# State-layer input weights turned by dense 64x64 products, inputs shifted by transfers, output products that ask for one head at a time, wider planner lags

## The chip, the cores and the metric

The kernel runs on one NeuronCore of a Trainium2 chip. The metric is device time in microseconds (us), and lower is better. The engines named here are TensorE (PE, with its weight loads as PEld), VectorE (DVE), ScalarE (ACT), GpSimd (POOL) and SyncE (SP, which issues the transfers). "att", "acc" and "big" are banks of PSUM, where products land.

## The reference

One layer for 256 tokens of width 2048, in float32. The state layer, which the change is about, is one of three mixers that read one projection:

```python
h = rmsnorm(x, norm_mix_pre)
q_na, k_na, v_na, u_ssm, q_mem = split(h @ w_in)
y_na  = neighbourhood_attention(q_na, k_na, v_na, rpb)       # 8 heads x 128
y_ssm = s5_mixer(u_ssm, ...)                                 # 32 groups of 16 channels, 64 complex states
y_mem = memory_cross_attention(q_mem, mem, ...)              # 4 heads x 128
# s5, each direction: bu = u @ b_bar ; h_t = lam_bar * h_(t-1) + bu_t (a scan over 256 steps) ; y = Re(c h)
y = concat(rmsnorm(y_na), rmsnorm(y_ssm), rmsnorm(y_mem))
x = x + rmsnorm(y @ w_out)
x = x + rmsnorm(square(relu(rmsnorm(x) @ w_ff1)) @ w_ff2)
```

## The kernel before

**The weight stream.** All dense weights lie in one stream of 128x1024 chunks (512 KB), in the order of their use. SP loads a chunk into `wraw` (three buffers); ScalarE rounds it to `wh` (conv_high), VectorE forms the rest `wl` (conv_low), and TensorE multiplies with both, three products for each of the reference's. `take` hands TensorE the next columns; it has the chunk two ahead converted, and a conversion issues the load of the chunk three further on. Chunks 0 to 15 are the first part of `w_in`, 16 to 31 `w_mem_kv`, 32 to 79 values, queries and keys of the neighbourhood heads, from 80 on `w_out`, then the MLP. A chunk of `w_mem_kv` is 12 products with the weight as stationary operand (into two banks), then 6 with `memS` as stationary operand.

**The planner.** There is no dynamic scheduler. While the program is written out, a clock for each engine is advanced by estimated costs. The side work lives in generators (`spawn`). At every half chunk `take` calls `tick`, which steps those that are due, and so puts their instructions between the products of the stream. After a step a task is due again when the engine it used is expected to be done plus a lag, `LAG[min(pri, 2)]`. `drain` steps one task until it is done. Every engine then runs its instructions strictly in the order that came out, so a wait of one instruction holds up all behind it on that engine.

**The state layer.** The 256 steps are cut into 64 blocks of four. `g0_evac` writes the input `uT` with VectorE and shifts it into `U4`, whose partitions hold the four steps of a block. For each of four groups `ut`, `prep_b` builds on VectorE the input weights times four powers of lambda (`W`). For each direction `d` it spreads them into `wx` (ScalarE; one half of the channels is zero), turns them on TensorE by 8 transposes of 128x128 (one pass each in the trace) and copies them to `W1T` (ScalarE). `incr` multiplies W1T with U4: 32 products of 128 rows by 32 columns with 64 moving columns, four column strips at a time (`tile_position=(0, 32 * m)`). A float32 product that is no transpose has two records, so an increment shows as x64. `XS` takes the result, `tree` scans it on VectorE, `ssm_out` multiplies with `CC`.

**The attention heads and the output projection.** `att_task` runs one head in steps (scores, softmax, `PT`, values). `na_fin` turns finished heads into `mixn`. The output projection first takes the memory heads (`mixm`, four groups of two chunks), then `drain(nf)` steps the other tasks until all eight heads stand in mixn, then come four groups over mixn.

Of the kernel before, what the change touches and what calls it, by code (L numbers as in the profile page):

```python
# [11 lines left out]
F32 = mybir.dt.float32  # L12
# [15 lines left out]
MEMH = 4  # L28
EPS = 1e-6
LAM_RE_MAX = -1e-4  # L30
NB = S // 4
LEV = 6
SCALE = 128 ** -0.5
# [4 lines left out]
HALF = DFF // 2 // 128  # L38
LASTK = 12
MARGIN = 200.0  # L40
LAG = (1200.0, 2000.0, 800.0)
SH_V = 1e9
SH_G = 500.0
BACK_V, BACK_G, BACK_A, BACK_TREE = 2600.0, 4000.0, 3000.0, 1700.0
# [59 lines left out]
def hybrid_kernel(ctx: ExitStack, tc: tile.TileContext, A: dict, out: bass.AP, dbg=None):  # L104
# [16 lines left out]
    class Engine:  # L121
# [3 lines left out]
        def __getattr__(self, name):  # L125
            f = getattr(self.raw, name)
            e = self.e

            def call(o, *a, **kw):
                n = 1  # L130
                for d in o.shape[1:]:
                    n *= d
                if e == "E":
                    m = a[0].shape[-1]
                    if name == "transpose":
                        c = 110.0
                    elif a[0].dtype == F32R:
                        c = n * 0.4225
                    else:
                        c = max(n, 128) * 1.69 * (0.31 if m == 32 else 1.0) if n > 4 else 110.0  # L140
                elif name == "tensor_reduce":
                    c = 80 + 1.04 * a[0].shape[1] * a[0].shape[2]
                elif e == "A":
                    c = (205 + 0.83 * n + (80 if isinstance(kw.get("scale"), bass.AP) or "bias" in kw else 0)
                         + (186 if "accum_out" in kw else 0))
                elif e == "V":
                    c = (72 if n > 64 else 140) + n * {"tensor_copy": 0.52, "reciprocal": 8.0, "tensor_tensor_scan": 1.04,
                                   "tensor_scalar": 0.76, "memset": 0.3}.get(name, 1.04)
                else:
                    c = 155 + n * {"tensor_scalar": 0.9, "memset": 0.0, "tensor_copy": 1.6}.get(name, 2.1)  # L150
                if e == "V" and n > 64 and name == "tensor_tensor" and any(
                        abs(x.ap[-1][0]) >= 4 for x in (o, a[0]) if x.ap[-1][1] > 1):
                    c += 0.9 * n
                book(e, c)
                return f(o, *a, **kw)  # L155
            return call
# [83 lines left out]
    def live(gen):  # L240
        return any(t[1] is gen for t in tasks)
# [18 lines left out]
            while more and all(clk[e.upper()] - clk["E"] < BACK[e] for e in t[3]):  # L260
                more = step(t)

    def drain(g):
        while live(g):
            me = next(t for t in tasks if t[1] is g)
            was = dict(clk)
            clk["E"] = max(clk["E"], me[2])
            step(me)
            if clk == was:
                for t in list(tasks):  # L270
                    if t is not me:
                        step(t)
                if clk == was:
                    clk["E"] += 500.0
# [383 lines left out]
    uT = a2.tile([128, 4, 256], F32, name="uT")  # L658
    U4 = a2.tile([128, 16, NB], F32, name="U4")

    wx = a2.tile([128, 8, 4, 2, 16], F32, name="wx")
    V.memset(wx.rearrange("p n l j b -> p (n l j b)"), 0.0)

    loaded = {}

    def load_b(ut):
# [5 lines left out]
    def prep_b(ut):  # L672
        yield from until(lambda: ut in loaded and clk["E"] > loaded[ut][1])
        raw = loaded[ut][0]
        w = a2.tile([128, 2, 2, 4, 4, 16], F32, name="W", tag="W", bufs=1)
        par = a2.tile([128, 4, 2, 2, 4], F32, name="par", tag="par", bufs=1)
        for i, x in enumerate((cfr, cfi, lbr, lbi)):
            act(par[:, i], x[:, 8 * ut:8 * ut + 8].rearrange("p (d q) -> p d q", d=2)[:, :, None, :]
                .to_broadcast([128, 2, 2, 4]))
        yield from done("A")  # L680
        for l in range(4):
            o = w[:, :, :, :, l, :]
            src = (w[:, :, :, :, l - 1, :].rearrange("p d c q b -> p (d c q) b") if l
                   else raw.rearrange("p (n b) -> p n b", b=16))
            r_, i_ = (par[:, 2 * min(l, 1) + i].rearrange("p d c q -> p (d c q)")[:, :, None].to_broadcast([128, 16, 16])
                      for i in range(2))
            t = a2.tile([128, 2, 2, 4, 16], F32, name="pt", tag="pt", bufs=1)
            tt(V, t.rearrange("p d c q b -> p (d c q) b"), src, i_, mult)
            tt(V, o.rearrange("p d c q b -> p (d c q) b"), src, r_, mult)
            tt(V, o[:, :, 0], o[:, :, 0], t[:, :, 1], sub)  # L690
            tt(V, o[:, :, 1], o[:, :, 1], t[:, :, 0], add)
            yield True
        yield from done("V")
        act(W0[ut].rearrange("p d c q j b -> p (d c q) j b"),
            w[:, :, :, :, 0, :].rearrange("p d c q b -> p (d c q) b")[:, :, None, :].to_broadcast([128, 16, 2, 16]))
        w0_done.add(ut)
        if ut % 2 == 0:
            XS[ut // 2] = a2.tile([128, 2, 16, NB], F32, name="XS", tag="AB", bufs=2)
        for d in range(2):
            for j in range(2):  # L700
                h = slice(64 * j, 64 * j + 64)
                act(wx[h, :, ::-1 if d == 0 else 1, j, :], w[h, d].rearrange("p c q l b -> p (c q) l b"))
            yield PE
            wt = a2.tile([128, 2, 4, 128], F32, name="W1T", tag="W1T", bufs=2)
            ps2 = [att(), att()]
            for n in range(8):
                PE.transpose(ps2[n // 4][:, n % 4 * 128:(n % 4 + 1) * 128], wx[:, n].rearrange("p l j b -> p (l j b)"),
                             ident)
            for c in range(2):
                act(wt[:, c].rearrange("p q m -> p (q m)"), ps2[c])  # L710
            spawn(incr(ut, d, wt, clk["A"] + MARGIN + LAG[2]), 2, "A")
            yield True

    def incr(ut, d, wt, t0):

        yield from until(lambda: ssm_done and clk["E"] > t0 and (d == 0 or (ut, 0) in xs_part))
        p = att()
        X = p.rearrange("p (c q m) -> p c q m", c=2, q=4)
        for c in range(2):
            for q in range(4):  # L720
                for m in range(4):
                    PE.matmul(X[32 * m:32 * m + 32, c, q, :], wt[:, c, q, 32 * m:32 * m + 32], U4[:, 4 * ut + q, :],
                              start=True, stop=True, skip_group_check=True, tile_position=(0, 32 * m))
        c0 = 8 * (ut % 2) + 4 * d
        act(XS[ut // 2][:, :, c0:c0 + 4, ::-1 if d else 1], X)
        xs_part.add((ut, d))
        yield
# [251 lines left out]
    def g0_evac():  # L979
        b = st_rx["b"]  # L980
        for j in range(2):
            tt(V, qkm[:, 2 * j:2 * j + 2, 0, :], pq[j].rearrange("p (a b) -> p a b", a=2),
               b[:, None, :].to_broadcast([128, 2, 256]), mult)
        yield
        for u in range(4):
            tt(V, uT[:, u].rearrange("p (r c) -> p c r", c=16),
               pu[:, u * 256:(u + 1) * 256].rearrange("p (c r) -> p c r", c=16), b.rearrange("p (c r) -> p c r", c=16),
               mult)
        yield
        for q in range(4):  # L990
            for i in range(4):
                o = U4[32 * i:32 * i + 32, q:16:4, :]
                s = uT[32 * q:32 * q + 32, :, i * NB:(i + 1) * NB]
                if i % 2:
                    G.tensor_copy(o, s)
                else:
                    act(o, s)
            if q < 3:
                yield True
        ssm_done.append(1)  # L1000
        if dbg:
            dbg("uT", uT.rearrange("p a b -> p (a b)"))
        yield
# [93 lines left out]
    acc1 = a1.tile([128, 2, D], F32, name="acc1", tag="x16", bufs=2)  # L1097
    mixn = a1.tile([128, 2, NAH, 256], F32R, name="mixn", tag="x16", bufs=2)

    def na_fin():  # L1100
        for h in range(NAH):
            yield from wait_for(naT[h])
            yield from split_task(mixn[:, 0, h, :], mixn[:, 1, h, :], yna[:, h, :], col(V_NA, h))

    def na_rms():
        yield from wait_for(nf)
# [3 lines left out]
    nf = spawn(na_fin(), pri=1)  # L1110
    nr = spawn(na_rms(), pri=1)

    def out_group(mh, ml, n):

        po = [acc(), acc()]
        for k in range(n):
            wh, wl = take(4)
            for t in range(2):
                s = slice(t * 128, (t + 1) * 128)
                mm_tok(po[t], mh[:, k, s], ml[:, k, s], wh, wl, start=(k == 0), stop=(k == n - 1))  # L1120
        return po
# [4 lines left out]
    for o in range(4):  # L1126
        po = out_group(mixm[:, 0], mixm[:, 1], 4)
        for t in range(2):
            act(acc1[:, t, quarter(o)], po[t], AF.Copy, scale=st_rx["mo"][:, t:t + 1])
    drain(nf)  # L1130

    mixs = {}

    def glu():
        yH, yL = yHL["H"], yHL["L"]
# [35 lines left out]
    for o in range(4):  # L1171
# [2 lines left out]
            gl = glu()  # L1174
        if o == 2:
            drain(nr)
        p1 = spawn(post1(o, out_group(mixn[:, 0], mixn[:, 1], NAH)), 1)
    drain(p1)
    drain(gl)
    A2.close()  # L1180
# [363 lines left out]
```

## Time and profile before

| | |
|---|---|
| median of 3 runs (lowest, highest) | 1140.99 us (1138.22, 1141.76) |
| the profiled execution, its span | 1140.01 us, 1138.2 us |
| busy share PE, DVE, ACT, POOL | 98%, 63%, 51%, 9% |
| bytes read from HBM | 209.02 MB |

The program is the same in every run. Of the span, about 417 us are the mixers and the output projection, which the change touches, and about 704 us the MLP, which it leaves as it was. In the rows below a product is written out<-in by the program's names; "U" is U4, "x" is x1. Loads of `x` and `gpost` are 256 KB each.

### The profile page before, as it was taken

What the parts mean: (1) busy time and instruction counts of PE and PEld (TensorE: products, weight loads), DVE (VectorE), ACT (ScalarE), POOL (GpSimd) and SP (SyncE); (2) the same over time, 40 slices, a digit from 0 to 9 for tenths busy, and PEclk for the clock granted to TensorE, in tenths of its full rate; (3) what the DMA queues carried; (4) which work ended last, traced back from release to release, by engine and by line L of the source; (5) the groups of instructions that cost most, each with busy time, mean ns of one, the idle gap of its engine ahead of it and who ended that gap; (6) DMA issues with size and microseconds to landing.
All of it is one profiled execution on the core that took longest, in us unless ns stands there. A gap on an engine that the chain in (4) does not pass through costs nothing.

```text
span 1138.2 us, 18307 instructions
## 1 busy us (share of the span) xinstructions
PE 1111.2 (98%) x7208; PEld 957.6 (84%) x7208; DVE 721.3 (63%) x1069; ACT 578.3 (51%) x900; POOL 104.8 (9%) x179
## 2 busy tenths in 40 slices
PE   8999999899999999999999999999999999999996
PEld 8988899799788878888888888888888888888885
DVE  6777588888876776866664444445666665445454
ACT  6567856636655464644455434434444444344341
POOL 1780000020110161000000000000000000001010
PEclk9999999999999999999999999999999999999999
DMA  9876444345455766666666666666666666666663
GB/s 302 291 254 184 127 145 142 114 140 166 135 148 179 249 188 181 189 191 191 187 186 193 189 189 186 186 187 192 193 186 189 191 191 187 186 198 195 193 209 129
DMA packets 62726, 212.31 MB, mean 187 GB/s; under 512 B 7216, under 2 KB 9776, under 8 KB 62640
## 3 DMA queue, kind: packets, MB, share of 16 engines
q1 hardware_dynamic: 62352, 211.05, 60.5%
q8 instruction: 56, 0.92, 0.3%
q14 instruction: 30, 0.25, 0.1%
q10 hardware_dynamic: 288, 0.09, 0.0%
HBM read 209.02 MB, written 2.10 MB: 185 GB/s over the span
## 4 chain that ended last, share of the span: by engine, by line
PE 83%; DVE 7%; DMA 3%; ACT 3%; issue 2%; POOL 1%; SPq 0%; DVEq 0%; POOLq 0%; ACTq 0%
PE acc L155 74%; PE big L155 6%; PE att L155 4%; DMA wraw<-in_w_dram 3%; DVE wl L155 3%; ACT wh L155 1%; DVE ps L155 1%; DVE W L155 1%; DVE XS L155 1%; ACT P L155 0%; DVE pt L155 0%; DVE mn L155 0%; DVE P L155 0%; POOL x L155 0%; DMA gpost<-in_post_dram 0%
## 5 line engine op out<-in xcount | busy, mean ns | idle before, releaser
L155 DVE TENSOR_TENSOR wl<-wraw,wh 128x1024 fp32r<-128x1024 f32 (+1 forms) x372 | 458.3, 1234 | 374.9 <-ACT wh L155 374.3
L155 ACT ACTIVATE wh<-wraw 128x1024 fp32r<-128x1024 f32 (+1 forms) x372 | 391.4, 1054 | 440.5 <-PE acc L155 275.3
L155 PE MATMUL acc<-hs,wh 128*128 128x512 f32 (+1 forms) x996 | 345.9, 391 | 0.0
L155 PE MATMUL acc<-hs,wl 128*128 128x256 f32 x992 | 279.3, 282 | 0.0
L155 PEld LDWEIGHTS acc<-hs,wh 128*128 128x128 f32 x996 | 186.6, 188 | 38.8 <-ACT hs L155 0.2
L155 PEld LDWEIGHTS acc<-hs,wl 128*128 128x128 f32 x992 | 187.3, 189 | 0.0
L155 PE MATMUL acc<-wh,fH 128*128 128x512 f32 x448 | 178.7, 399 | 0.0
L155 PE MATMUL acc<-wh,fL 128*128 128x512 f32 x448 | 176.5, 394 | 0.0
L155 PE MATMUL acc<-wl,fH 128*128 128x512 f32 x448 | 175.7, 392 | 0.0
L155 PEld LDWEIGHTS acc<-wh,fL 128*128 128x128 f32 x448 | 84.1, 188 | 22.0
L155 PEld LDWEIGHTS acc<-wl,fH 128*128 128x128 f32 x448 | 84.1, 188 | 19.9
L155 PEld LDWEIGHTS acc<-wh,fH 128*128 128x128 f32 x448 | 84.1, 188 | 19.4
L155 PE MATMUL acc<-xH,wh 128*128 128x256 f32 x256 | 74.4, 291 | 0.0
L155 PE MATMUL acc<-xH,wl 128*128 128x256 f32 x256 | 72.0, 281 | 1.4 <-DVE wl L155 1.4
L155 PE MATMUL acc<-xL,wh 128*128 128x256 f32 x256 | 71.9, 281 | 0.2 <-issue 0.2
L155 POOL TENSOR_TENSOR facc<-facc,g 128x512 f32<-128x512 f32 x6 | 9.3, 1572 | 474.8 <-DMA g<-in_g_dram 474.8
L155 PEld LDWEIGHTS acc<-xH,wl 128*128 128x128 f32 x256 | 48.3, 188 | 1.9 <-DVE wl L155 1.6
L155 PEld LDWEIGHTS acc<-xH,wh 128*128 128x128 f32 x256 | 48.3, 189 | 0.8
L155 PEld LDWEIGHTS acc<-xL,wh 128*128 128x128 f32 x256 | 48.4, 189 | 0.1
L155 PE MATMUL acc<-wh,mixn 128*128 128x512 f32 x128 | 41.0, 398 | 0.0
L155 ACT ACTIVATE P<-P,mn 128x160 f32<-128x160 f32 (+1 forms) x24 | 10.8, 449 | 46.0 <-DVE mn L155 46.0
L155 DVE TENSOR_TENSOR ps<-XS,pw 128x32 f32<-128x32 f32 (+9 forms) x44 | 30.1, 683 | 1.2
(307 smaller groups left out, 1481.8 us busy)
## 6 DMA issues: line engine op xcount, KB each, us to landing
wraw<-in_w_dram SPq DMA_DIRECT2D x369, 512.0 KB, 3.6
tokst<-in_xt_dram SPq DMA_DIRECT2D x4, 512.0 KB, 7.4
mst<-in_memT_dram SPq DMA_DIRECT2D x4, 512.0 KB, 5.5
tokst<-in_mt_dram SPq DMA_DIRECT2D x4, 512.0 KB, 5.3
x<-in_xt_dram SPq DMA_DIRECT2D x8, 256.0 KB, 5.3
out_dram<-facc SPq DMA_DIRECT2D x8, 256.0 KB, 2.5
xst<-in_xT_dram SPq DMA_DIRECT2D x7, 256.0 KB, 6.4
bias<-in_bias_dram SPq DMA_DIRECT2D x8, 160.0 KB, 3.6
```

Source lines behind the costliest of these rows:

```text
L155: return f(o, *a, **kw)
```

## The change

The turn of the input weights drops the zero half: the powers are laid out in a row `wf`, so that the 64 columns of one turn lie side by side, and each half of the channels is multiplied with the identity in its own 64x64 quadrant of TensorE, both into one bank. W1T is half as large, and `incr` works in the same two quadrants. U4 is filled by 32 transfers of 16 partitions x 4 x 64 elements (16 KB) in place of 16 copies on ScalarE and GpSimd, and the increments are free to be written out once the planner's clock is 6000 ns further. The groups over mixn ask for a head just ahead of its product, in place of the drain ahead of them. Two lags and two costs of the planner change.

```diff
@@ constants
-LAG = (1200.0, 2000.0, 800.0)
+WSTEP, WROW = 576, 1248
+LAG = (1200.0, 2600.0, 1600.0)
@@ cost of a TensorE instruction in the planner's clock
-                        c = 110.0
+                        c = 110.0 if n == 128 else 50.0
...
-                        c = max(n, 128) * 1.69 * (0.31 if m == 32 else 1.0) if n > 4 else 110.0
+                        c = max(n, 128) * 1.69 * (0.31 if m == 32 else 1.0 if m > 64 else 0.27) if n > 4 else 110.0
@@ drain
-    def drain(g):
-        while live(g):
+    def drain(g, enough=lambda: False):
+        while live(g) and not enough():
@@ state layer, before its tasks
-    wx = a2.tile([128, 8, 4, 2, 16], F32, name="wx")
-    V.memset(wx.rearrange("p n l j b -> p (n l j b)"), 0.0)
@@ prep_b
-        w = a2.tile([128, 2, 2, 4, 4, 16], F32, name="W", tag="W", bufs=1)
+        wf = a2.tile([128, WROW], F32, name="W", tag="W", bufs=1)
+
+        def power(l):
+            a, n = (3 - l) * 16, WSTEP + (2 * l - 3) * 16
+            return (wf[:, a:a + 2 * n].rearrange("p (d x) -> p d x", d=2)[:, :, 0:512]
+                    .rearrange("p d (n l b) -> p d n l b", n=8, l=4)[:, :, :, 0, :])
...
-        act(W0[ut].rearrange("p d c q j b -> p (d c q) j b"),
-            w[:, :, :, :, 0, :].rearrange("p d c q b -> p (d c q) b")[:, :, None, :].to_broadcast([128, 16, 2, 16]))
+        for d in range(2):
+            act(W0[ut][:, d].rearrange("p c q j b -> p (c q) j b"),
+                power(0)[:, d][:, :, None, :].to_broadcast([128, 8, 2, 16]))
...
+        yield from done("A")
         for d in range(2):
-            for j in range(2):
-                h = slice(64 * j, 64 * j + 64)
-                act(wx[h, :, ::-1 if d == 0 else 1, j, :], w[h, d].rearrange("p c q l b -> p (c q) l b"))
-            yield PE
-            wt = a2.tile([128, 2, 4, 128], F32, name="W1T", tag="W1T", bufs=2)
-            ps2 = [att(), att()]
+
+            wt = a2.tile([128, 2, 4, 64], F32, name="W1T", tag="W1T", bufs=2)
+            p = att()
             for n in range(8):
-                PE.transpose(ps2[n // 4][:, n % 4 * 128:(n % 4 + 1) * 128], wx[:, n].rearrange("p l j b -> p (l j b)"),
-                             ident)
-            for c in range(2):
-                act(wt[:, c].rearrange("p q m -> p (q m)"), ps2[c])
+                for j in range(2):
+                    h = slice(64 * j, 64 * j + 64)
+                    PE.matmul(p[h, 64 * n:64 * n + 64], wf[h, WSTEP * d + 64 * n:WSTEP * d + 64 * n + 64], ident[h, h],
+                              start=True, stop=True, skip_group_check=True, tile_position=(64 * j, 64 * j))
+            act(wt.rearrange("p c q m -> p (c q m)"), p)
@@ incr
-                for m in range(4):
-                    PE.matmul(X[32 * m:32 * m + 32, c, q, :], wt[:, c, q, 32 * m:32 * m + 32], U4[:, 4 * ut + q, :],
-                              start=True, stop=True, skip_group_check=True, tile_position=(0, 32 * m))
+                for j in range(2):
+                    h = slice(64 * j, 64 * j + 64)
+                    PE.matmul(X[h, c, q, :], wt[h, c, q, :], U4[h, 4 * ut + q, :], start=True, stop=True,
+                              skip_group_check=True, tile_position=(64 * j, 64 * j))
@@ g0_evac
         for q in range(4):
-            for i in range(4):
-                o = U4[32 * i:32 * i + 32, q:16:4, :]
-                s = uT[32 * q:32 * q + 32, :, i * NB:(i + 1) * NB]
-                if i % 2:
-                    G.tensor_copy(o, s)
-                else:
-                    act(o, s)
-            if q < 3:
-                yield True
+            for j in range(2):
+                for i in range(4):
+                    r = 64 * j + 16 * i
+                    nc.sync.dma_start(U4[r:r + 16, q:16:4, :],
+                                      uT[32 * q + 16 * j:32 * q + 16 * j + 16, :, i * NB:(i + 1) * NB])
+        yield from after(6000.0)
         ssm_done.append(1)
@@ output projection
+            na_done.add(h)
...
-    def out_group(mh, ml, n):
+    def out_group(mh, ml, n, ready=lambda k: None):
...
         for k in range(n):
+            ready(k)
             wh, wl = take(4)
...
-    drain(nf)
...
+    def head(h):
+        drain(nf, lambda: h in na_done)
...
-        p1 = spawn(post1(o, out_group(mixn[:, 0], mixn[:, 1], NAH)), 1)
+        p1 = spawn(post1(o, out_group(mixn[:, 0], mixn[:, 1], NAH, head)), 1)
```

The new costs and lags, the shorter hand-over and the fewer copies move nearly all side work in the mixer part. On SP, in the middle of `w_mem_kv` (wraw_1076 and wraw_1074 are the load of chunk 26), before:

```order
L319 DMA wraw_1032<-in_w_dram 128x1024
L458 DMA mst_1074<-in_memT_dram 128x1024
L319 DMA wraw_1076<-in_w_dram 128x1024
L319 DMA wraw_1117<-in_w_dram 128x1024
L319 DMA wraw_1144<-in_w_dram 128x1024
L319 DMA wraw_1176<-in_w_dram 128x1024
```

and of the change:

```order
L320 DMA wraw_1030<-in_w_dram 128x1024
L459 DMA mst_1072<-in_memT_dram 128x1024
L320 DMA wraw_1074<-in_w_dram 128x1024
L1000 DMA U4_112<-uT_111 16x4x64 x32
L320 DMA wraw_1145<-in_w_dram 128x1024
L320 DMA wraw_1182<-in_w_dram 128x1024
L320 DMA wraw_1217<-in_w_dram 128x1024
```

The 32 transfers into U4 now stand between the loads of chunks 26 and 27. On TensorE, in the middle of chunk 25 (wh_1140 before, wh_1178 of the change), before:

```order
L155 MATMUL acc_852<-memS_1137,wh_1140 128x256 x2
L155 MATMUL acc_852<-memS_1137,wl_1141 128x256
L155 MATMUL acc_853<-wh_1140,memS_1137 128x512
L155 MATMUL acc_853<-wl_1141,memS_1137 128x512
L155 MATMUL acc_853<-wh_1140,memS_1137 128x512
```

and of the change:

```order
L156 MATMUL acc_850<-memS_1175,wh_1178 128x256 x2
L156 MATMUL acc_850<-memS_1175,wl_1179 128x256
L156 MATMUL att_1306<-U4_112,W1T_1231 64x64 x16
L156 MATMUL att_1324<-U4_112,W1T_1250 64x64 x16
L156 MATMUL acc_851<-wh_1178,memS_1175 128x512
L156 MATMUL acc_851<-wl_1179,memS_1175 128x512
```

The first two increments, of both directions, stand here; the same place of chunk 24, 18 products earlier, has the 2 x 16 products of the first two turns. Before, the first turn stood in chunk 30 and the first increment in chunk 33. On ScalarE, around the conversions of chunks 27 and 28 (wh_1203 and wh_1234 before, wh_1284 and wh_1366 of the change), before:

```order
L155 ACTIVATE memS_1200<-mst_906,vecs_71 128x256
L155 ACTIVATE wh_1203<-wraw_1117 128x1024
L155 ACTIVATE U4_112<-uT_111 32x4x64 x2
L155 ACTIVATE memS_1231<-mst_1074,vecs_71 128x256
L155 ACTIVATE wh_1234<-wraw_1144 128x1024
```

and of the change:

```order
L156 ACTIVATE memS_1281<-mst_904,vecs_71 128x256
L156 ACTIVATE wh_1284<-wraw_1145 128x1024
L156 ACTIVATE CC_113<-Cw_889 64x64x16 x2
L156 ACTIVATE XS_1198<-att_1306 128x2x256
L156 ACTIVATE XS_1198<-att_1324 128x2x4x64
L156 ACTIVATE memS_1363<-mst_1072,vecs_71 128x256
L156 ACTIVATE wh_1366<-wraw_1182 128x1024
```

The copy into U4 is gone; between the two conversions stand the copies of the state weights into CC and those of the first two increments into XS. In the same way the scan on VectorE starts ahead of the conversion of chunk 36 rather than chunk 44, and the second group's weights are built behind that of chunk 27 rather than chunk 36.

## Rows read from the trace of the kernel before

**Rows 1.** The page: its first line and part 1 for TensorE.

```profile
span 1138.2 us, 18307 instructions
...
PE 1111.2 (98%) x7208; PEld 957.6 (84%) x7208; DVE 721.3 (63%) x1069; ACT 578.3 (51%) x900; POOL 104.8 (9%) x179
```

**Rows 2.** Busy time by stage; columns as the first line names them.

```profile
core 0: us, PE busy (x) PEld busy (x) DVE busy (x) ACT busy (x) POOL busy (x), PEclk, DMA share, GB/s
...
72.00:150.00 78.00, 77.20 (x745) 66.88 (x745) 55.69 (x104) 56.41 (x100) 11.23 (x21) 1.00 0.54 171
150.00:217.00 67.00, 61.31 (x621) 57.27 (x621) 54.97 (x105) 42.75 (x95) 2.74 (x6) 0.97 0.45 136
217.00:290.00 73.00, 72.78 (x888) 68.02 (x887) 62.64 (x105) 38.62 (x71) 9.28 (x11) 1.00 0.50 151
290.00:340.00 50.00, 46.84 (x507) 38.94 (x507) 38.69 (x65) 30.68 (x62) 4.67 (x8) 1.00 0.44 130
```

**Rows 3.** TensorE's waits: who for whom, us in total, times, longest.

```profile
PE acc L155 <- DVE wl L155: 4.7, 7, 1.4
...
PE att L155 <- ACT wx L155: 1.8, 1, 1.8
...
PE att L155 <- ACT W1T L155: 0.8, 1, 0.8
PE att L155 <- ACT PT L155: 0.8, 1, 0.8
```

**Rows 4.** Timeline of TensorE: one turn and one increment, each with the next product.

```profile
100.29 1.03 PE L155 MATMUL att<-ident,wx 128*128 128x128 f32 x8
101.08 0.49 PE L155 MATMUL acc<-memS,wh 128*128 128x256 f32 x2
...
140.84 1.10 PE L155 MATMUL att<-U,W1T 128*32 128x64 f32 x64
141.87 0.39 PE L155 MATMUL acc<-xH,wh 128*128 128x256 f32 x1
```

**Rows 5.** Timeline of SP: the load of chunk 26, and five issues in a row.

```profile
78.08 0.33 SPq L319 DMA_DIRECT2D wraw<-in_w_dram  x1
...
383.70 0.86 SPq L1185 DMA_DIRECT2D x<-in_xt_dram  x2
384.61 0.90 SPq L1198 DMA_DIRECT2D gpost<-in_post_dram  x2
385.55 0.59 SPq L1185 DMA_DIRECT2D x<-in_xt_dram  x1
```

**Rows 6.** The instructions of out_dram: the eight output transfers, issue to landing.

```profile
DMA to landing us min/median/max: 2.3/2.5/2.6
```

**Rows 7.** Timeline of ScalarE: the conversion of chunk 26.

```profile
84.14 1.06 ACT L155 ACTIVATE wh<-wraw 128x1024 fp32r<-128x1024 f32 x1 [3.23 <-DMA wraw<-in_w_dram]
```

**Rows 8.** Timeline of TensorE: the middle of chunks 24 and 25.

```profile
82.97 0.40 PE L155 MATMUL acc<-wh,memS 128*128 128x512 f32 x1
...
85.78 0.40 PE L155 MATMUL acc<-wh,memS 128*128 128x512 f32 x1
```

**Rows 9.** Timeline of TensorE: the two waits in one turn.

```profile
210.88 0.66 PE L155 MATMUL att<-ident,wx 128*128 128x128 f32 x4 [1.79 <-ACT wx L155]
212.28 1.11 PE L155 MATMUL att<-ident,wx 128*128 128x128 f32 x4 [0.75 <-ACT PT L155]
```

**Rows 10.** Busy time in two windows behind them (PEclk is the third number from the end).

```profile
212.00:214.00 2.00, 1.72 (x6) 1.57 (x7) 2.00 (x3) 1.77 (x4) 0.00 (x0) 0.52 0.00 0
214.00:216.00 2.00, 2.00 (x7) 1.59 (x6) 1.51 (x2) 0.14 (x2) 0.00 (x0) 0.62 0.85 242
```

**Rows 11.** Groups of instructions: ScalarE's copies into wx.

```profile
L155 ACT ACTIVATE wx<-W 64x512 f32<-64x512 f32 x16 | 10.0, 624 | 0.8 <-DVE W L155 0.6
```

**Rows 12.** The page, parts 5 and 6: a chunk's conversions and its load.

```profile
L155 DVE TENSOR_TENSOR wl<-wraw,wh 128x1024 fp32r<-128x1024 f32 (+1 forms) x372 | 458.3, 1234 | 374.9 <-ACT wh L155 374.3
L155 ACT ACTIVATE wh<-wraw 128x1024 fp32r<-128x1024 f32 (+1 forms) x372 | 391.4, 1054 | 440.5 <-PE acc L155 275.3
...
wraw<-in_w_dram SPq DMA_DIRECT2D x369, 512.0 KB, 3.6
```

More of the change, by code (lines that the diff above doesn't have):

```diff
@@ L681, in prep_b @@
         for l in range(4):
[L682 to L691, printed above, removed]
+            o = power(l)
+            src = power(l - 1) if l else raw.rearrange("p (d n b) -> p d n b", d=2, n=8)
+            r_, i_ = (par[:, 2 * min(l, 1) + i].rearrange("p d c q -> p d (c q)")[:, :, :, None]
+                      .to_broadcast([128, 2, 8, 16]) for i in range(2))
+            t = a2.tile([128, 2, 8, 16], F32, name="pt", tag="pt", bufs=1)
+            tt(V, t, src, i_, mult)
+            tt(V, o, src, r_, mult)
+            tt(V, o[:, :, 0:4], o[:, :, 0:4], t[:, :, 4:8], sub)
+            tt(V, o[:, :, 4:8], o[:, :, 4:8], t[:, :, 0:4], add)
             yield True
         yield from done("V")
-        act(W0[ut].rearrange("p d c q j b -> p (d c q) j b"),
-            w[:, :, :, :, 0, :].rearrange("p d c q b -> p (d c q) b")[:, :, None, :].to_broadcast([128, 16, 2, 16]))
+        for d in range(2):
+            act(W0[ut][:, d].rearrange("p c q j b -> p (c q) j b"),
+                power(0)[:, d][:, :, None, :].to_broadcast([128, 8, 2, 16]))
         w0_done.add(ut)
@@ L1098, in hybrid_kernel @@
     mixn = a1.tile([128, 2, NAH, 256], F32R, name="mixn", tag="x16", bufs=2)
+    na_done = set()
     def na_fin():
```

## The prediction

> **What bounds the kernel now.** I read the page first: TensorE is busy for 1111.2 of the 1138.2 us span [rows 1]. Whatever takes its time or makes it wait is on the path; whatever shortens another engine counts only where TensorE waits for it. The profiled execution took 1140.01 us, 1.8 us more than its span and 1.0 us below the median of 1140.99.
>
> Then the stages [rows 2]. The diff touches only the mixer half, before about 340 us. There TensorE is idle for 0.8 us (72 to 150), 5.7 us (150 to 217), 0.2 us (217 to 290) and 3.2 us (290 to 340), 9.9 us in all: this is what better placed work could win, besides TensorE's own time. The list of waits says for whom [rows 3]: 4.7 us for the low halves of the weights on VectorE over the whole kernel, 1.8 us for the copies into `wx`, 0.8 us for `W1T`, 0.8 us for a bank that `PT`'s copy frees. The wx, W1T and PT waits are the only ones here with the name of something that the diff removes or shortens. The longest stands at 210.88, followed by another at 212.28 [rows 9], and behind them the granted clock is 0.52 and 0.62 for two windows of 2 us, that is, between its levels of 2.4 and 1.2 GHz [rows 10]. That costs 2 x 0.48 + 2 x 0.38 = 1.7 us more.
>
> **The turn of the input weights.** Before, one direction of one group costs TensorE 8 transposes of 128x128, 0.79 us from 100.29 to 101.08 [rows 4]. After, it costs 16 products of a 64x64 quadrant with the identity, each in two passes: 32 passes over 64 columns. No row has a quadrant. The nearest is the old increment: 64 passes over 64 columns, four 32-column strips side by side, in 1.03 us [rows 4], so 16 slots of 64 ns. If two quadrants on the diagonal also run side by side, the new turn needs 16 slots, 1.03 us; one after the other it needs 2.06 us. Eight of them cost 8 x 0.24 = 1.9 us more, or 10.2 us.
>
> **The increment.** 32 products of 128x32 become 16 of 64x64: again 16 slots if two run at once (1.03 us as now, nothing won), or 32 slots (8.2 us more over the eight). I take side by side for both, since the strips in rows 4 plainly do so. Together **+1.9 us**, and +18.4 us at the other end.
>
> **What leaves ScalarE, GpSimd and VectorE.** The 16 copies into wx (10.0 us, [rows 11]), half of the W1T copies, the 16 copies into U4 and a memset go. All this lies beside TensorE's products, so it is worth nothing except where TensorE waits for it: the 1.8 us for wx, the 0.8 us for W1T and, since the bank wait sits in the middle of such a turn, the 0.8 us for PT, with the 1.7 us of half clock behind them: 5.1 us. Of the other idle time of these stages (0.8 + 2.3 + 0.2 us, what is left of 5.7 after the 3.4) I give the wider lags and the emptier ScalarE queue half, 1.6 us. **-6.7 us** together. The bounds: nothing, if other waits take the places of these, as a reordered program has new neighbours everywhere; and 11.6 us, if all 9.9 us of idle time and the 1.7 us go.
>
> **One head at a time.** The four mixm groups no longer end with all attention heads emitted at once. The 3.2 us of idle time there [rows 2] hang on weight conversions behind ScalarE's evacuations, which stay; I take 0, and 3.2 us is in the bound above.
>
> **The 32 transfers into U4.** This is where I see the largest term, and it is a loss. They are issued by SP, in order, behind the load of chunk 26 and ahead of that of chunk 27, and the first increment now follows in the middle of chunk 25. In the trace of before:
> - SP issues chunk 26 at 78.08 [rows 5]. Nothing earlier on SP changes, so the transfers start after that.
> - Each transfer takes the next of eight semaphores and waits until the transfer eight places before it has landed. The eighth waits for chunk 26, which lands just before ScalarE starts on it at 84.14 [rows 7].
> - From there 24 are still to be issued. Issues that follow each other directly stand 0.46 us apart: five from 383.70 to 385.55 [rows 5]. So the last is issued at 84.1 + 24 x 0.46 = 95.1. The shortest landing shown, of the output, is 2.3 to 2.6 us [rows 6]: it lands at 97.6. If issuing cost nothing, the semaphores would still allow eight per landing: 84.1 + 4 x 2.5 = 94.1. If chunk 26 landed in the usual 3.6 us [rows 12], at 81.7, that chain would end at 91.7.
> - TensorE comes to the increment at 85.78, plus two turns put in at 82.97 [rows 8], 2.06 us: 87.8.
>
> So TensorE waits 97.6 - 87.8 = 9.8 us; the bounds are 3.9 us and, at 0.60 us an issue (the last in rows 5, 0.59 long), 13 us. I take 9.8, since 0.46 is what SP does with transfers that follow each other. TensorE has then stood still for longer than at 210.88, so I add the same 1.7 us of half clock. **+11.5 us.**
>
> The Trainium skill speaks against this part too: "DMA: Bandwidth & Descriptors", section Rules for kernel authors, says that many small transfers should be made one large one, and that under 64 KB one pays mostly overhead. These are 16 KB each (16 partitions of 4 x 256 B). No run here shows a transfer so small; by the rule the sum stays as it is.
>
> What queues behind: on SP the load of chunk 27, issued at 95.6 instead of 79.95. With 3.6 us to land, 1.05 us on ScalarE and 1.23 us on VectorE [rows 12] it is ready at 101.5; TensorE, resumed at 97.6, has two increments (2.1 us) and one and a half chunks (4.2 us) to do and wants it at 103.9. So it is just hidden, and becomes a second wait if TensorE resumes before about 95. On ScalarE the copy of the increment into XS stands behind chunk 27's conversion, and chunk 28's behind it: late, but no later than TensorE.
>
> **Sum.** 1140.0 + 1.9 - 6.7 + 11.5 = 1146.7; 1.0 more against the median. I predict **1147 us**, against 1141.
>
> **Rivals.**
> - *The transfers are quick enough* (faster). If short transfers are issued and landed much quicker than any row shows, so that the last lands by 88 to 90, the place costs 0 to 2 us and no clock: 1140.0 + 1.9 - 6.7 + 1 = 1136. For it: 16 KB is an eighth of the smallest load. Against it: the issue times here do not shrink with size (256 KB loads 0.46 apart, 512 KB ones 0.33 long alone), and the landing chain alone gives 91.7. It decides below a cost of 1.4 us in all; at 4.8 us the change breaks even. Chance 0.20.
> - *Every wait goes.* The state layer now starts some eight chunks earlier, and with that all 9.9 us and the 1.7 us could go: 1140.0 + 1.9 - 11.6 + 11.5 = 1141.8, no change. Against it: VectorE, behind 4.7 us of the waits, gets little less to do. Chance 0.18.
> - *The quadrants do not overlap.* All terms as above, but the products cost 18.4 us, and TensorE comes 2.1 us later to the increment: 1140.0 + 18.4 - 6.7 + 11.5 - 2.1 = 1161. Both quadrants of a pair write the same PSUM bank, in different partitions; the strips of rows 4 do that too, but read all 128 rows. Chance 0.10. The Trainium skill has it as a rule: "TensorEngine Tiling (Array Packing)", section Restrictions and Gotchas, says that different row tiles cannot use one PSUM bank at the same time. No row here has row tiles, so the trace neither agrees nor disagrees.
> - *My forecast*, the wait with moderate gains, 1142 to 1153: chance 0.52.
>
> **Chances and range.** Less than 0.3% (3.4 us) is about what a measurement of this kernel cannot tell from no change: 1137.6 to 1144.4. Faster: the quick transfers' 0.17 and 0.03 of the second rival, 0.20. Same: 0.13 of the second rival, 0.03 of the first, 0.08 of mine, 0.24. Slower: 0.56. The range leaves out most of the third rival and the best cases of the first: 1134 to 1156; my own case alone is 1142 to 1153.
>
> **What would show it.** Right: SP issuing 32 U4 transfers for over 10 us from about 78; a TensorE wait of 4 to 13 us for a DMA into U4 ahead of att<-U4,W1T near 88; the clock below 1 right behind; no wait for wx. A turn that takes 1.0 us from its start to the next product's, or 2.1, settles the quadrants. I am wrong if that wait is under 2 us, or if idle time in 217 to 340 grows by more than 4 us, which I price at nothing.

## The result and the profile after

The changed kernel took 1146.35 us (median of 4 runs, 1145.56 to 1147.59), the kernel before 1139.76 beside it: ratio 1.0058, 95% interval 1.0036 to 1.0080, slower by 0.4 to 0.8%. The profiled execution took 1145.56 us; it stands against the 1140.01 us of the kernel before.

The page's first lines and part 1 for TensorE, which answer to [rows 1]:

```profile
span 1143.8 us, 18188 instructions
...
PE 1113.1 (97%) x7144; PEld 962.5 (84%) x7144; DVE 717.4 (63%) x1068; ACT 563.6 (49%) x872; POOL 103.1 (9%) x171
```

The span grew by 5.6 us, and TensorE's busy time by only 1.9: the loss is idle time. Busy time by stage, columns as in [rows 2]:

```profile
72.00:150.00 78.00, 67.37 (x615) 57.45 (x615) 52.92 (x101) 42.83 (x81) 6.89 (x13) 0.93 0.47 144
150.00:217.00 67.00, 67.00 (x714) 64.64 (x713) 57.88 (x105) 36.60 (x74) 2.88 (x4) 1.00 0.49 151
217.00:290.00 73.00, 73.00 (x814) 67.54 (x814) 64.55 (x118) 44.38 (x89) 9.92 (x11) 1.00 0.50 150
290.00:340.00 50.00, 49.60 (x546) 43.29 (x545) 31.13 (x38) 28.64 (x54) 6.19 (x10) 1.00 0.52 161
340.00:417.00 77.00, 73.49 (x362) 59.97 (x361) 52.41 (x96) 38.11 (x63) 11.78 (x10) 1.00 0.63 198
```

The last row of the kernel before, which [rows 2] does not have:

```profile
340.00:417.00 77.00, 75.60 (x383) 62.37 (x381) 53.82 (x85) 41.00 (x68) 14.82 (x14) 1.00 0.65 207
```

Both signs of the forecast are here. Between 150 and 340 us the idle time of TensorE fell from 9.1 us to 0.4, and from 72 to 150 it rose from 0.8 to 10.6. From 340 to 417, which the forecast left out, it rose from 1.4 to 3.5. The list of TensorE's waits says what for, columns as in [rows 3]:

```profile
PE att L156 <- DMA U<-uT: 9.9, 5, 2.4
...
PE acc L156 <- DVE wl L156: 1.6, 2, 0.8
PE acc L156 <- DVE half L156: 1.4, 1, 1.4
PE acc L156 <- DVE memS L156: 1.2, 1, 1.2
PE acc L156 <- DVE mixn L156: 1.0, 1, 1.0
```

The waits for wx, W1T and PT are gone. New are 9.9 us for the transfers into U4, and 2.4 us for `half` and `mixn` in the output projection. SP's timeline, in the place of [rows 5], and the group of the 32 issues (ns min/median/max, first and last start):

```profile
77.24 0.33 SPq L320 DMA_DIRECT2D wraw<-in_w_dram  x1
77.63 21.48 SPq L1000 DMA_DIRECT2D U<-uT  x32
99.22 6.54 SPq L320 DMA_DIRECT2D wraw<-in_w_dram  x4
```

```profile
L1000 SPq DMA_DIRECT2D U<-uT x32: 585/593/970, 77.6 to 98.5; - x32
...
DMA to landing us min/median/max: 1.8/1.9/5.3
```

For 21.5 us SP issues nothing but these, one every 0.67 us; the load of chunk 27 leaves at 99.22. TensorE in the meantime:

```profile
83.67 2.08 PE L156 MATMUL att<-ident,W 64*64 64x64 f32 x64
85.68 0.50 PE L156 MATMUL acc<-wh,memS 128*128 128x512 f32 x1
...
88.70 0.44 PE L156 MATMUL att<-U,W1T 64*64 64x64 f32 x6
90.29 0.30 PE L156 MATMUL att<-U,W1T 64*64 64x64 f32 x2 [1.16 <-DMA U<-uT]
92.94 0.30 PE L156 MATMUL att<-U,W1T 64*64 64x64 f32 x2 [2.35 <-DMA U<-uT]
...
100.50 3.00 PE L156 MATMUL att<-U,W1T 64*64 64x64 f32 x50 [2.01 <-DMA U<-uT]
103.43 0.60 PE L156 MATMUL acc<-wh,memS 128*128 128x512 f32 x1
...
130.11 2.08 PE L156 MATMUL att<-U,W1T 64*64 64x64 f32 x64
132.12 0.91 PE L156 MATMUL att<-CC,W 128*32 128x96 f32 x32
```

The first increment starts at 88.70 and then goes on transfer by transfer, at SP's pace: two passes (one product of a quadrant), then a wait of about 2 us. A product reads what four transfers bring, and four issues are 4 x 0.67 = 2.7 us, the step from 90.29 to 92.94. The next product of the stream starts at 103.43, 14.7 us after the first increment; two increments take 2.0 us elsewhere in this trace (130.11 to 132.12), so the place costs **12.7 us**. The granted clock, windows around it:

```profile
92.00:94.00 2.00, 0.30 (x2) 0.19 (x2) 0.00 (x0) 0.00 (x0) 0.00 (x0) 0.86 0.13 25
94.00:96.00 2.00, 0.45 (x2) 0.29 (x2) 0.00 (x0) 0.00 (x0) 0.00 (x0) 0.50 0.14 26
...
100.00:102.00 2.00, 1.50 (x28) 1.53 (x30) 0.00 (x0) 0.00 (x0) 0.00 (x0) 0.50 0.83 191
102.00:104.00 2.00, 2.00 (x30) 1.84 (x27) 0.00 (x0) 0.92 (x1) 0.00 (x0) 0.58 1.02 404
```

It stands at the lower level (0.50) through most of the standstill and for 3 us after it, so that the last 50 passes took 2.9 us, where 64 take 2.0 at the higher one.

### The profile page after: what moved, and what is told of

Read it like the earlier page. It is cut to its first block, busy times and chain, and to the rows that moved or that the text cites. A ratio compares the mean times of both kernels' runs of the same rounds, so it can differ in the third digit from the quotient of the medians.

```text
span 1143.8 us, 18188 instructions
## 1 busy us (share of the span) xinstructions
PE 1113.1 (97%) x7144; PEld 962.5 (84%) x7144; DVE 717.4 (63%) x1068; ACT 563.6 (49%) x872; POOL 103.1 (9%) x171
## 4 chain that ended last, share of the span: by engine, by line
PE 86%; DMA 3%; DVE 3%; POOL 3%; issue 2%; SPq 1%; ACT 1%; DVEq 0%; POOLq 0%; ACTq 0%
PE acc L156 77%; PE big L156 5%; PE att L156 5%; DMA wraw<-in_w_dram 3%; SPq L1000 1%; DVE wl L156 1%; ACT wh L156 1%; POOL u L156 1%; DVE W L156 0%; POOL cs L156 0%; POOL x L156 0%; DMA gpost<-in_post_dram 0%; POOL q L156 0%; POOL t L156 0%; POOL acc L156 0%
## 5 line engine op out<-in xcount | busy, mean ns | idle before, releaser
L156 PEld LDWEIGHTS acc<-wh,mixn 128*128 128x128 f32 x128 | 23.9, 188 | 8.8 <-DVE half L156 1.8
```

## The experiments

Two theories stood against each other. *A, the transfers:* the 32 issues on SP cost by what waits for them, the increments on TensorE and the next weight load behind them on SP. *The rivals:* the loss lies in the increments' early place alone (B), or in the new order of the program, and the standstill itself bought the quiet stages behind it (C). "Before" in the ratios is the kernel before, run on the same chip in the same rounds. The shorter of the edits are shown; none leaves any of the computation out. Differences to the changed kernel are between medians of different rounds; the kernel before lay between 1139.76 and 1140.79 in them, so a difference of about 1 us there cannot be told from none.

**Increments later (late).** The transfers stay where they are.

```diff
-        yield from after(6000.0)
+        yield from after(30000.0)
         ssm_done.append(1)
@@ prep_b, so that no third W1T is asked for ahead of the first increment
+        yield from until(lambda: ut == 0 or (ut - 1, 1) in xs_part)
```

(The second edit alone leaves the changed kernel's order as it is.)

> The changed kernel, with the increments free to be written out 30000 ns after the transfers in place of 6000: the first two stand in chunk 31 instead of chunk 25; the 32 transfers stay between the loads of chunks 26 and 27 on SP. Theory A, the queue: SP is taken for 21.5 us by the issues, so that the load of chunk 27 starts at 99.2 whoever reads U4, and it is ready at 105.4. TensorE, that no longer stops in chunk 25, comes to chunk 27 at about 92.9 and waits there for some 11 us and at half clock behind: 1144 to 1149, no change against the changed kernel's 1146. Rival B, the reader: the time is lost because the increments stand too close behind the transfers: 1145.6 - 12.9 = 1133.

Measured: 1153.88 us, ratio 1.0117 (1.0103 to 1.0131), 7.5 us slower than the changed kernel. One timeline row of SP and the first row of TensorE's waits:

```profile
77.81 22.91 SPq L1001 DMA_DIRECT2D U<-uT  x32
```

```profile
PE acc L156 <- ACT wh L156: 13.9, 1, 13.9
```

Rival B falls. No increment waits any more; the wait is now for `wh` of chunk 27, whose load leaves at 100.82. It ends at 106.0. Theory A named the place but put too little on it (1144 to 1149): the wait was 13.9 us and not 11, and the waits for `wl` elsewhere are 5.1 us where the changed kernel has 1.6.

**Another queue, nothing else (pool_close), and another queue with later increments (pool).**

```diff
-                    nc.sync.dma_start(U4[r:r + 16, q:16:4, :],
+                    nc.gpsimd.dma_start(U4[r:r + 16, q:16:4, :],
@@ pool only, with the edit in prep_b shown above
-        yield from after(6000.0)
+        yield from after(45000.0)
```

> The changed kernel with nothing else edited than the queue of the 32 transfers: GpSimd's in place of SP's; the first increments stay in chunk 25. In the run with GpSimd's queue and late increments the issues went from 76.2 to 95.1. Theory A2: the transfers cost in two places, each enough by itself: the reader (an increment ahead of the last landing) and SP (the load of chunk 27 behind them). Here the second is gone and the first stays: TensorE waits from 88.7 to about 97, 7 to 9 us with half clock behind, 1142 to 1145. Rival B2: only SP's hold-up costs, and increments wait little: 1133 to 1136.

> The 32 transfers go to GpSimd's queue in place of SP's, and the increments are free 45000 ns later (first two in chunk 31). Theory A: SP is free for the loads, nothing waits, and the 9.9 us of wait and 3 us at half clock and around go: 1145.6 - 12.9 = 1133, with the load of chunk 27 issued at about 80. Rival C: the standstill of TensorE in the changed kernel gave ScalarE and VectorE time to run ahead, and part of the idle time that is gone after 150 us comes back without it: 1136 to 1141. Rival D: GpSimd issues a transfer much slower than SP's 0.67 us, or the transfers land after chunk 31: a wait for U4 on TensorE at about 104, over 1141.

Measured: pool_close 1141.80 us, ratio 1.0010 (1.0001 to 1.0018); pool 1135.29 us, ratio 0.9951 (0.9938 to 0.9963). The issues and the wait of pool_close:

```profile
L1000 POOL DMA_DIRECT2D U<-uT x32: 514/514/746, 75.1 to 94.0; - x32
...
DMA to landing us min/median/max: 1.7/3.7/5.9
```

```profile
PE att L156 <- DMA U<-uT: 6.7, 5, 2.7
```

```profile
78.23 0.33 SPq L320 DMA_DIRECT2D wraw<-in_w_dram  x1
```

GpSimd issues hardly faster than SP (0.61 us from one to the next), so TensorE, at the increments from 87.05 on, still waits 6.7 us, a little less than theory A2 gave. But the load of chunk 27 leaves at 78.23, right behind that of chunk 26, as before the change. So the reader and the loads behind the transfers are two costs, each enough by itself: with the first alone 1141.8, with the second alone 1153.9, with both, largely at the same time, 1146.35, with neither 1135.3 in pool. (The four differ in the order of their side work too, so these are no terms to add up.) The time of pool lies between theory A (1133) and rival C (1136 to 1141): another wait has come up, read from its list of waits:

```profile
PE att L156 <- issue: 4.6, 1, 4.6
```

It stands from 108.6 on, between two sets of products of CC with W that the planner had put side by side. ScalarE, in order, first empties the first set's bank (eight small copies, 2.27 us) and only then copies CC for the second (2.12 us, to 113.08); TensorE goes on at 113.18.

**The transfers in small portions on SP (spread).** One transfer at each of the planner's ticks, in a task of its own; the increments follow in chunk 45. The edit in prep_b shown above is here too.

```diff
+    def u4_task():
+        for q in range(4):
+            for j in range(2):
+                for i in range(4):
...
+                    yield
+        yield from after(6000.0)
+        ssm_done.append(1)
...
+        spawn(u4_task(), 1)
```

> The 32 transfers stay on SP, but are written out one at a time, one or two behind each load from chunk 27 to chunk 48; the first increments stand in chunk 45. Theory A: SP has 2.8 us a chunk and needs 0.33 + 2 x 0.67 = 1.7, so no load is late: about 1133 as without the wait. Rival C (what the standstill gave is lost): 1136 to 1141. Rival E: the scan and what follows start twenty chunks later than in the changed kernel and come late for the output projection: idle time for yH or mixs behind 340 us, over 1141.

Measured: 1137.79 us, ratio 0.9979 (0.9969 to 0.9989): the wait is gone on SP too, 8.6 us of gain over the changed kernel. One load and one portion in its trace:

```profile
89.12 0.33 SPq L320 DMA_DIRECT2D wraw<-in_w_dram  x1
89.50 0.59 SPq L990 DMA_DIRECT2D U<-uT  x1
```

It stays 8.5 us behind the best version below, at a time that rival C had forecast (1136 to 1141); what speaks against C comes with pool26. Part of it shows where rival E looked, though mostly for another tile: 2.7 us of waits for `mixn` from 318 on, and 0.7 us for `yH`. That the late scan on VectorE is what delays mixn was not tried by itself.

**The quadrants one after the other (serial).** Loops exchanged in the turn and in the increment.

```diff
-            for n in range(8):
-                for j in range(2):
+            for j in range(2):
+                for n in range(8):
@@ incr
-        for c in range(2):
-            for q in range(4):
-                for j in range(2):
+        for j in range(2):
+            for c in range(2):
+                for q in range(4):
```

> The changed kernel with the loops of the turn and of the increment exchanged: all products of the first quadrant, then all of the second, in place of the two by turns. The same products, the same data. Theory F: two quadrants run side by side only where they follow each other; then a turn and an increment take 2.0 us each instead of 1.0, over eight of both 16 us: 1162. Rival G: what was measured as 1.0 us is the rate of one quadrant, and nothing runs side by side: no change, 1146.

Measured: 1156.49 us, ratio 1.0140 (1.0125 to 1.0156), 10.1 us slower than the changed kernel. Two turns at full clock, with the product behind them; the changed kernel's two turns are at 83.67 above:

```profile
124.25 3.40 PE L156 MATMUL att<-ident,W 64*64 64x64 f32 x64
127.58 0.50 PE L156 MATMUL acc<-wh,memS 128*128 128x512 f32 x1
```

3.33 us against 2.01 for the same 64 passes, on average 52 ns for a pass against 31. The single records of the two traces, which these rows merge, show how. In the changed kernel the passes of the two quadrants start 6 to 7 ns apart, and the next two 58 ns after them. In serial the next pass of the same quadrant starts 58 ns after the last; only at a change of quadrant do three passes start within 6 ns of one of the other. Theory F holds, and G falls. F's size was off: 58 ns and not the 64 ns that I had from the strips of [rows 4], and the overlap at the changes. With the rows above it is 8 x 2 x 0.66 = 10.6 us, against the 10.1 measured.

**Only the transfers (before_c).** The kernel before, its 16 copies into U4 replaced by 16 transfers of 32 KB.

```diff
-                if i % 2:
-                    G.tensor_copy(o, s)
-                else:
-                    act(o, s)
-            if q < 3:
-                yield True
+                nc.sync.dma_start(U4[32 * i:32 * i + 32, q:16:4, :],
+                                  uT[32 * q:32 * q + 32, :, i * NB:(i + 1) * NB])
```

> The kernel before, with the copies into U4 on ScalarE and GpSimd replaced by 16 transfers on SP of 32 partitions x 4 x 64 elements (32 KB), between the loads of chunks 26 and 27; the turn, the increments, the lags and the output products as before. The first increment then stands in chunk 26, as a copy no longer has to be waited for. Theory A: 16 issues of 0.6 to 0.67 us take SP for 10 us, the load of chunk 27 starts at about 88.5 and is ready at 95; TensorE comes to it at about 94 to 95, so a wait of at most 2 us there and at most 1 us for U4: 1140 to 1143. Rival H: an issue costs by its rows (128 here, 64 in the changed kernel), so about twice as long: 20 us, and the same loss as in the changed kernel: 1150. Rival I: free of cost: 1140 or, with the earlier start, below.

Measured: 1143.76 us, ratio 1.0030 (1.0019 to 1.0041). SP's timeline, then the first wait of TensorE's list, then the two rows of ScalarE that explain it:

```profile
77.56 11.36 SPq L992 DMA_DIRECT2D U<-uT  x16
89.02 6.84 SPq L319 DMA_DIRECT2D wraw<-in_w_dram  x4
```

```profile
PE att L155 <- ACT W1T L155: 5.4, 2, 4.7
```

```profile
93.19 1.06 ACT L155 ACTIVATE wh<-wraw 128x1024 fp32r<-128x1024 f32 x1 [8.47 <-DMA wraw<-in_w_dram]
94.15 1.07 ACT L155 ACTIVATE W1T<-att 128x512 f32<-128x512 f32 x2
```

Half as many transfers of twice the size take half the time to issue, 0.59 to 0.60 us each in both kernels: an issue is paid by the transfer and not by its rows, and rival H falls. The wait is named for W1T, but W1T's copy was only queued on ScalarE behind the conversion of chunk 27, which sat idle for 8.47 us until its late load landed. It is the late load again, under another name than in late. Theory A had priced this wait at 2 us at most and overlooked that order; it was 4.7, and a wait of 2.7 us at 100.5 for a copy into XS, further down the same queue, follows it.

**The lags, the heads (before_de, drain, lag).** before_de makes only these two edits to the kernel before; drain puts `drain(nf)` back ahead of the output projection's mixn groups, and lag the old `LAG`, both in the changed kernel.

> The kernel before, with the wider lags and the output products that ask for one head at a time, without the turn, the increment and the transfers of the change. The prediction's terms: 1.6 us for the lags, 0 for the heads: 1138. Rival J: the whole gain that the changed kernel shows beside the transfers (1145.6 - 12.9 = 1132.7 against 1140.0, that is 7.3 us) is one of the order of the program: 1132 to 1134. Rival K: nothing from either, 1140.

> The changed kernel, with all eight heads emitted ahead of the first product over mixn, as before. The changed kernel has waits of 1.0 us for mixn and 1.4 us for the half ahead of it at 342 and 346, where the kernel before had none of this name and 0.9 us more for weight conversions from 310 to 340. Theory L: one head at a time costs these 2.4 us: 1143 to 1144. Prediction's term: 0, 1146.

> The changed kernel with the lags of before (2000 and 800 in place of 2600 and 1600). The first increments then stand half a chunk earlier, so TensorE waits 1.4 us longer for U4; the other increments two to three chunks earlier. Prediction's term: the wider lags are worth up to 1.6 us, so 1147 to 1149. Rival: nothing, 1146, or the later waits for W1T and PT of before come back: up to 1150.

Measured: before_de 1139.20, ratio 0.9989 (0.9981 to 0.9998), a gain of about 1.5 us (0.2 to 2.2 by the interval), so rival J falls. drain 1144.51, ratio 1.0033 (1.0021 to 1.0045), 1.8 us better than the changed kernel: one head at a time costs here, theory L. The waits for `half` and `mixn` are absent from its list. In its trace TensorE comes to the first increment at 87.28, 1.4 us earlier than in the changed kernel, and yet the last wait for U4 ends at 100.58, 0.1 us later: who comes earlier waits longer (11.1 us here), and SP sets the end. lag 1152.44, ratio 1.0102 (1.0088 to 1.0116), 6.1 us worse than the changed kernel and above all that had been expected for it. The first row of its waits against the changed kernel's 9.9:

```profile
PE att L156 <- DMA U<-uT: 12.3, 7, 2.2
```

About 2 us of the 6.1 are U4's, since the increments stand half a chunk earlier: the last wait ends at 101.17 instead of 100.50, and half a chunk, 1.4 us, is then still to do that the changed kernel has behind it. The rest is spread over waits of up to 1.8 us: for weight conversions most of all (4.1 us for `wl` in acc against 1.6, and 2.9 for `wh`, which the changed kernel's list does not have), and for qk and for ScalarE's BD, which are not in that list either.

**What beats both (pool20, pool26, pool20_heads).** GpSimd's queue and the edit in prep_b, with the increments free after 20000 or 26000 ns, so that the copy into CC stands ahead of both sets of products. pool20_heads is pool20 with all heads ahead of the mixn groups.

> GpSimd's queue, and the increments free after 20000 ns: first two in chunk 28, which TensorE reaches at about 97 to 98, about when the last transfer lands. In the run with 45000 ns two sets of products of CC with W stood together and TensorE waited 4.6 us at 108 for ScalarE's copy into CC; here they stand apart, with the copy ahead of both. Theory A: no wait for U4 over 1 us, none at 108: 1130 to 1132. Rival: another wait takes the place of that one: 1134 to 1137.

> GpSimd's queue, and the increments free after 26000 ns: first two in chunk 31, the copy into CC ahead of both sets of products. Theory A: 1130 to 1132; nothing waits for U4. Rival: a new wait in the place of the one at 108, 1134 to 1137.

> As the run with 20000 ns, and all eight attention heads emitted ahead of the products over mixn, as in the kernel before. In the changed kernel that was worth 1.8 us (1144.5 against 1146.35). Theory L: 1.5 to 2 us below the run with 20000 ns. Rival: the wait of 0.7 us for mixn, which the run with GpSimd's queue still had, is all there is to win: under 1 us.

Measured: pool20 1133.40, ratio 0.9934 (0.9921 to 0.9948); pool26 **1129.34**, ratio 0.9896 (0.9883 to 0.9910); pool20_heads 1132.38, ratio 0.9923 (0.9911 to 0.9936). pool20 still waits 1.6 us for U4, and lies between theory A and its rival. In pool26 the increments come in chunk 31; its list of TensorE's waits, up to the last that the mixers have:

```profile
PE acc L156 <- DVE BD L156: 2.5, 1, 2.5
PE acc L156 <- DVE wl L156: 2.2, 3, 1.0
PE acc L156 <- DVE memS L156: 1.2, 1, 1.2
PE big L156 <- DVE wl L156: 1.1, 2, 0.8
...
PE acc L156 <- DVE mixn L156: 0.7, 1, 0.7
```

No wait for U4, none by the CC copies, none for wx, W1T, PT or qk. It is 17.0 us faster than the changed kernel and 11.5 faster than the kernel before. The stages behind the increments, columns as in [rows 2]:

```profile
150.00:217.00 67.00, 67.00 (x891) 64.29 (x890) 57.43 (x94) 35.02 (x74) 4.29 (x7) 1.00 0.47 138
217.00:290.00 73.00, 72.02 (x731) 67.67 (x721) 62.17 (x112) 42.32 (x85) 7.70 (x10) 1.00 0.52 158
290.00:340.00 50.00, 49.26 (x371) 40.58 (x371) 28.77 (x44) 30.80 (x53) 5.10 (x8) 1.00 0.53 155
340.00:417.00 77.00, 75.48 (x401) 63.53 (x400) 54.53 (x91) 43.37 (x74) 24.10 (x22) 1.00 0.66 210
```

Rival C falls with it: without the standstill the stages behind are as quiet (3.2 us idle from 150 to 417, the changed kernel 3.9). It even comes out 4.3 us below the 1133.6 that is left when 12.7 is taken off the changed kernel's 1146.35; where these 4.3 us come from stays open. pool20_heads is 1.0 us below pool20, between theory L and its rival, and the runs of the two overlap: what one head at a time costs there stays open within 0 to 2 us.

## Why the prediction was right

Forecast 1147 (1134 to 1156), measured 1146.35: the mechanism, its place and the side were right. That the number came so close is in part luck, since the three terms missed by -0.4, +1.2 and -1.9 us. (There is a slip in the sum: 1146.7 and the 1.0 us against the median make 1147.7 and not 1147.) By its steps, against the profiled execution (5.6 us more than before):

- **Products, +1.9 forecast.** Two turns take 2.01 us (83.67 to 85.68), 1.0 each as forecast, against 0.79: 8 x 0.21 = 1.7. Two increments elsewhere in the trace (130.11 to 132.12) take the same 2.01 us, against 1.03 each before: -0.2. Together +1.5. The rival of quadrants that do not overlap falls by the run serial. Both quadrants of a pair write one bank here, in different partitions; what I quoted from the Trainium skill, "TensorEngine Tiling (Array Packing)", Restrictions and Gotchas, is not seen in this form: their passes start 6 to 7 ns apart, and a pair takes the 58 ns of a pass alone.
- **U4, +11.5 forecast, 12.7 measured.** The wait is 9.9 us where I had 9.8, but the sizes under it were off and cancelled, which is luck. The issues stand 0.67 us apart and not 0.46: the row of loads that I took the pace from was no guide to transfers of this kind, and even the 0.60 of my upper bound was too low. From the landing of chunk 26 (82.8), 24 x 0.67 gives 98.9 for the last issue (98.5 measured), with 95.1 forecast. Against that, a transfer landed in 1.9 us instead of 2.5, TensorE came to the increment at 88.7 instead of 87.8, and 14 of its 64 passes fit between the waits. What is left beside the wait is 2.8 us (12.7 - 9.9). The lower clock is 1.7 of it, as forecast: the last 50 passes took 2.9 us where 1.6 would do, and two of the products between the waits 0.45 instead of 0.30. The other 1.1 I did not have: a product by itself between two waits is busy for 0.30 us, where its two passes have a share of 0.06 in a row of 64.
- **Chunk 27 just hidden.** Right: the changed kernel has no wait for its conversion, and the run late shows it as a wait as soon as the increments stand elsewhere.
- **Waits removed, -6.7 forecast.** What is left of the 5.6 after 1.5 and 12.7 is -8.6, within the bounds of 0 and -11.6. The waits for wx, W1T and PT and the half clock behind are all gone, and with them nearly all other idle time between 150 and 340, of which I had given half. The new waits behind 340 are in the -8.6 too, so what was won is more.
- **Lags and heads.** I had 1.6 for the lags with the emptier ScalarE, and 0 for the heads; before_de measured 1.5 for lags and heads in the kernel before. In the changed kernel the lags are worth 6.1 us and one head at a time costs 1.8, by medians of different rounds. The second is a term that I put at nothing with the argument that the evacuations stay; what it brings is that VectorE forms a head's low half (`mixn`) only when TensorE already asks for it, the waits of 1.0 and 1.4 us that end at 343.2 and 347.7. (The second is listed under `half`, a memset of 0.06 us right behind that step on VectorE.)
- **Small transfers.** The rule that I cited from the Trainium skill, "DMA: Bandwidth & Descriptors", Rules for kernel authors, agrees in its direction: 16 transfers of 32 KB took SP 11.4 us, 32 of 16 KB 21.5. U4 in transfers of over 64 KB was not tried. (The smallest loads of the kernel before are 44 and 48 KB, on ScalarE's queue, and not the 128 KB that "an eighth" took for it; no term rested on that.)

What stays open is how the 8.6 us divide between the turn, the emptier ScalarE and the new order: before_de (1.5 us for lags and heads together) and lag (6.1 us for the lags alone) suggest that a part is worth more or less by the order that it stands in, so a sum over parts has no fixed terms here.

## What to carry to other kernels

A transfer costs its issue on the queue that it stands on, here the same 0.6 us for 16 KB and for 32 KB; 32 of them in a row ahead of a stream of loads are a stop of 21 us for the stream. Before moving work to such a queue, ask two questions apart: who reads the result, and what is queued behind; curing one alone moved the wait to the other (1153.9) or left more than half of what could be won (1141.8), and curing both, with the increments in a good place, turned a loss of 0.6% into a gain of 1.0%. The name in a list of waits is that of the last thing on the chain: the same late load showed as `wh` in late and as `W1T` in before_c.

## What the runs showed of the hardware that was not expected

- SP takes longer to issue a 16 KB or 32 KB transfer between places of SBUF (0.59 to 0.60 us) than a 512 KB load from HBM (0.33 us), and GpSimd takes 0.51 us for the same 16 KB transfer. What makes the difference is not shown: a 256 KB load of `x` from HBM took SP 0.59 us too [rows 5].
- A 16 KB transfer landed in 1.9 us (median) in the changed kernel, where no load left SP meanwhile, against 2.5 for the output's 256 KB in [rows 6]. On GpSimd's queue it took 3.5 to 3.9 us, but there the weight loads ran beside it, and it took as long on SP in spread, between loads. So the queue is not shown to be the cause. The row of spread:

```profile
DMA to landing us min/median/max: 2.8/3.9/6.0
```

- In a quadrant of 64x64 a float32 pass over 64 columns starts 58 ns after the last. Two quadrants on the diagonal by turns start 6 to 7 ns apart and need the same 58 ns for the pair, while both write one PSUM bank; at the lower clock level (0.50, the 50 passes from 100.50 on) a pair takes 107 ns.
